# Two matrix-product stages of a two-layer trunk: upper pools on 128-byte multiples, buffers and transposes placed anew

## The chip, the core and the metric

The kernel runs on one core of a Trainium2 chip, in one launch. The metric is the device time of that launch in microseconds (us). The engines are TensorE (PE in the profile; PEld is its loading of stationary operands), VectorE (DVE), ScalarE (ACT), GpSimd (POOL) and SyncE (SP, which issues nearly all DMAs).

## What is computed

One streaming step of a two-layer encoder, for 1024 prompt tokens and 128 sample tokens of width 1024: nine blocks of 128 rows, the ninth being the sample's. Layer 0 (L0) mixes with a gated linear recurrence, layer 1 (L1) with differential attention; each is followed by the same MLP. All is float32.

```python
for l in range(DEPTH):                                    # 2
    a = _rmsnorm(h, norm_g[l, 0])
    m = ...                                               # recurrence or attention, then @ w_o
    h = h + _rmsnorm(m, norm_g[l, 1])
    f = jnp.square(jax.nn.relu(_rmsnorm(h, norm_g[l, 2]) @ w_up[l])) @ w_down[l]   # 1024x4096, 4096x1024
    h = h + _rmsnorm(f, norm_g[l, 3])
```

The attention's own projections read `_rmsnorm(h)` of L0's result; the output of L1 is returned.

## The kernel before

**Products.** Each float32 operand is split in two: a high part in the type fp32r (an ACT cast) and the rest (a DVE subtraction). A product is three matmuls: high by high, high by low, low by high (`mm3`, L228). Wide matmuls have 512 columns, pj and pi 256, pq and pf 384. An operand in the text is named by the tile: h or l at the end is the high or the low part.

**Stages.** On L0: recurrence, `out_proj` (L596), `mlp_up` (L675), `mlp_down` (L851); on L1: attention, `out_proj`, `mlp_up`, `mlp_down`. In the profiled execution they begin at about 0, 630, 760, 1145, 1558, 2140, 2240 and 2622 us.

**Pools.** `Area` (L69) opens one tile pool for each name of a list. Pools without a side are stacked from the low end of the SBUF upwards (lower pools), those with `side="right"` from the high end downwards (upper pools). A pool of a later stage lies over bytes of an earlier one, and a tile's first use waits for the last reader of what it lies over. aTh and aTl (lower, all stages) hold the transposed input of the products, by block; in down they are the places of its operands.

**out_proj** takes the blocks in the order SOON (L0) or LATE (L1): products pm of a block, then its norm (`rstd_of` L184, with rs_v at L193), the residual (hb, loaded and stored by SP), the second norm, transposes of t by PE (`half_T` L225 to L232) whose results ACT and DVE copy out. As soon as blocks j and j+4 are there, `pair_sums` (L660) makes four sums of their halves, on POOL, for the last block on DVE (L667), and transposes one. The last block in both orders is a prompt block (7); the sample (8) stands sixth.

**mlp_up** multiplies by Strassen's scheme with seven products: P1 to P7, 12 matmuls each, over pairs of column tiles, 16 steps i in all. The sums of weights are POOL's (`sums`); `split` makes the stationary operands s0 (raw weights) and s1 (sums), upper, and, from the second step on in turn, s2, lower. Operands A11, A12, A22 and S2 are slices of aTh and aTl, the others (a1, a3, a4) upper tiles that the op `ops` of the first step makes by transposes. `smp` is the sample's product U (24 matmuls of 256 columns). Results (c) go through relu and square to DRAM (u_dr). The order in the first step is written out by hand:

```python
seq = "P1 smp P2 ops P6 P5 P7 P3 P4" if i == 0 else "P1 P6 P2 P5 P7 smp P3 P4"
```

X, Y, Z and U are PSUM tiles in pools of two banks each.

**mlp_down** runs seven passes in the order P1 P2 P5 P3 P6 P7 P4, over 8 chunks c each (4 in P4, whose rest goes block by block). A chunk is 4 blocks x 2 x 3 = 24 matmuls D of 512 columns, in P1, P2, P5 and P3 also 6 matmuls S for the sample. After each chunk the operands of later ones are made: `h_load` (SP, five chunks ahead) and `h_split` (hst to aTh, aTl: ACT L865, DVE L866), `w_load` and `w_split` (wsta, wstb to wh, wl; where the operand is a sum T1 to T4, POOL subtracts first, L934). hst, wh and wl are upper, wsta and aO lower. `evac` (L963) takes the results out of PSUM into aO and aE: ACT in the first four passes, DVE in P6, P7, P4 (L974 to L980), with two sums on POOL in P6.

**finish** (L942) of a block makes norm, residual and store. On L0 it then scales it (ACT, L263) and at once puts 8 transposes S into PE's order, which fill aTh and aTl for the attention. Blocks 0 to 3 are finished at every second chunk of P7, the sample's at the second chunk of P6, blocks 4 to 7 in the second half of P4 right behind their D products. POOL multiplies some of them by the gain gb (L952).

**Attention** begins with the projections pj of the keys, whose weights go through the ring wst, whi, wlo (`load_w` L155, upper; the query weights through the same wst, with a scaling by POOL). PE's order is the order of issue; each engine works its own instructions in order.

Of the kernel before, what the change touches and what calls it, by code (L numbers as in the profile page):

```python
# [19 lines left out]
P = 128  # L20
# [38 lines left out]
LATE = (0, 4, 1, 5, 2, 8, 3, 6, 7)  # L59
SOON = (0, 1, 2, 3, 4, 8, 5, 6, 7)  # L60
# [8 lines left out]
def tile_kernel(ctx, tc, x_prompt, x_sample, cache_k, cache_v, state_hgrn, norm_g, w_hgrn_in,  # L69
# [61 lines left out]
    aTl = glob.tile([P, NB, KT, P], F32R, name="aTl")  # L131
    rings = [ExitStack()]
# [450 lines left out]
    def prepare(ob, b, o_src, osc, gain, pp):  # L583

        nc.sync.dma_start(out=ob, in_=o_src[b * P:(b + 1) * P, :])
        rs = osc(ob, b, pp)
# [9 lines left out]
    def out_proj(w, gains, gain, o_src, osc, g_post, h_old, h_new, g_pre, order, W=None, early={}):  # L596

        keep = ExitStack()
        ts, blk = Area(keep, "ts", "t"), {}
        with ExitStack() as os_:  # L600
# [9 lines left out]
            def prep(b):  # L610
                if b not in early:
                    prepare(block(b), b, o_src, osc, gain, pp)

            order = LATE if early else SOON
# [7 lines left out]
            for b in order:  # L622
# [8 lines left out]
                if early.get(b) is not None:  # L631
                    ss = pp.tile([P, 2], F32, name="ss2")
# [4 lines left out]
                    rs = rstd_of(ss[:, 0:1], 1, 1.0 / D, pp)  # L637
# [4 lines left out]
                else:  # L642
                    rs = rstd_of(sumsq(pm, t, pp), 1, 1.0 / D, pp)
# [5 lines left out]
                pre_norm(hb, g2, t, t, pp, b)  # L649
# [4 lines left out]
                if b < NBP and b ^ NP in done:  # L654
                    pair_sums(blk, b % NP, nc.vector if b == order[-1] else nc.gpsimd)
# [19 lines left out]
    def mlp_up(l, blk, keep):  # L675
        wu = w_up[l].rearrange("(k p) n -> p k n", p=P)
        with ExitStack() as ms, ExitStack() as ls:
            R = Area(ms, "ur", "wst s0h s0l s1h a1h a1l a3h a3l s1l a4h a4l p1 u2 u3 c0 hs", side="right")
            B = Area(ms, "ub", "X Y Z U", space=PSUM)
# [4 lines left out]
            def bank(tag):  # L684
                return B.tile([P, 512], F32, name=tag)
# [80 lines left out]
            tset = split(st, 1, [(r1, ca), (r0, ca)])  # L766
            pend = None
            for i in range(NFP):
                sets = (raw, tset)
                X, Y, Z, U = None, None, None, None  # L770
                nx = None
                C = {}
                seq = "P1 smp P2 ops P6 P5 P7 P3 P4" if i == 0 else "P1 P6 P2 P5 P7 smp P3 P4"
                for op in seq.split():
                    if op == "P1":
# [4 lines left out]
                        nx = load(i + 1) if i + 1 < NFP else None  # L780
                    elif op == "P2":
# [4 lines left out]
                        store(c, "A11", i)  # L786
                    elif op == "ops":
# [62 lines left out]

    def mlp_down(l, g_post, h_old, h_new, last):  # L851
        wd = w_down[l].rearrange("(i s p) n -> s p i n", s=2, p=P)
        NC = NFP // 2
        with ExitStack() as ms:
            L = Area(ms, "dl", "wsta sst ysm aO")
            R = Area(ms, "dr", "aE wstb jk ss rs_v rs_y rs_t hst wh wl gb hb", side="right")
# [3 lines left out]
            ysm = L.tile([P, 2, 512], F32, name="ysm", bufs=1)  # L860
            gp = nc.gpsimd.tensor_tensor
            vt = nc.vector.tensor_tensor

# [10 lines left out]
            def h_load(n):  # L874
# [3 lines left out]
                hraw[n] = st = R.tile([P, 2, HT] if p < 7 else [P, NFP // 2, P], F32, tag="hst", name="hst", bufs=3)  # L878
# [7 lines left out]
            def h_split(n):  # L886
# [8 lines left out]
                if p < 4:  # L895
                    st = L.tile([P, 2, P], F32, name="sst", bufs=2)
# [14 lines left out]
            def w_get(n, c, x):  # L911
                st = (L if x == "a" else R).tile([P, 2, 512], F32, name="wst" + x, bufs=3 if x == "a" else 2)
# [14 lines left out]
            def w_split(m):  # L927
# [12 lines left out]
            gain = []  # L940

            def finish(b, y):  # L942
# [527 lines left out]
```

## Time and profile before

| what | value |
|---|---|
| median of three runs (lowest, highest) | 3015.61 us (3014.43, 3019.21) |
| the profiled execution | 3016.47 us |
| its span | 3014.8 us |
| mean granted clock of PE | 0.978 |
| busy: PE, PEld, DVE, ACT, POOL | 95%, 83%, 62%, 40%, 27% |
| share of PE in the chain that ended last | 85% |

The span is what the profiler saw of the program, from the first instruction to the last; the difference of 1.67 us lies around it. A share is busy time over the span. The granted clock is what the throttle gave of 2.4 GHz: 1 is full speed, and in a stretch a value between 0.5 and 1 is a mix of the two levels 2.4 and 1.2 GHz. The duration printed for a matmul is longer than the distance to the next one's start, since matmuls overlap.

### The profile page before, as it was taken

The numbers are of one execution on the slowest core, as the hardware profiler recorded it, in microseconds if no ns is written. First come the engines' busy times: TensorE is split into PE (matmuls) and PEld (weight loads), VectorE is DVE, ScalarE is ACT, GpSimd is POOL, SyncE is SP. The second block draws the span as 40 slices with busy tenths as digits, with TensorE's granted clock in tenths as the row PEclk, the third lists the DMA queues.
The fourth block names the chain that finished last, engine by engine and source line by source line (L and its number), as shares of the span: only waits on it lengthen the run. The fifth ranks groups of instructions, "written<-read, shape, count | busy, mean of one in ns | idle before, by whom it ended". The sixth has DMA issues, their size and how long they took to land.

```text
span 3014.8 us, 45342 instructions
## 1 busy us (share of the span) xinstructions
PE 2869.3 (95%) x16897; PEld 2500.1 (83%) x16897; DVE 1866.6 (62%) x3440; ACT 1195.5 (40%) x2566; POOL 803.3 (27%) x618
## 2 busy tenths in 40 slices
PE   7999999979899998999779999999989999999997
PEld 7999999968788886888669999998778888788876
DVE  7777777766644445555954665656675444456576
ACT  4232232333433334443444555556533333344432
POOL 1111111101545440114522110111134544302263
PEclk9999999979999999999989999999999999999999
DMA  4111121142243348678732121312323334577866
GB/s 135 53 52 52 52 58 53 56 148 84 76 150 128 125 152 279 193 264 273 259 113 72 53 75 52 91 52 79 125 105 109 134 125 150 192 240 253 266 228 220
DMA packets 337120, 405.27 MB, mean 134 GB/s; under 512 B 21081, under 2 KB 210690, under 8 KB 336898
## 3 DMA queue, kind: packets, MB, share of 16 engines
q1 hardware_dynamic: 336898, 402.37, 40.5%
q8 instruction: 133, 2.18, 0.3%
q14 instruction: 89, 0.73, 0.1%
HBM read 280.12 MB, written 122.16 MB: 133 GB/s over the span
## 4 chain that ended last, share of the span: by engine, by line
PE 85%; DVE 6%; issue 3%; DMA 3%; ACT 2%; POOL 1%; SPq 0%; ACTq 0%; DVEq 0%; POOLq 0%
PE D L228 17%; PE pj L228 10%; PE Y L228 8%; PE Z L228 6%; PE X L228 5%; PE S L228 3%; PE U L228 3%; PE pi L272 2%; PE pi L271 2%; PE pi L273 2%; PE sc L228 2%; PE po L228 2%; PE pm L271 2%; PE pm L273 2%; PE pm L272 2%
## 5 line engine op out<-in xcount | busy, mean ns | idle before, releaser
L228 PE MATMUL D<-wh,aTh 128*128 128x512 f32 x896 | 359.8, 402 | 27.6 <-ACT aTh L865 15.7
L228 PE MATMUL D<-wl,aTh 128*128 128x512 f32 x896 | 358.2, 400 | 6.0 <-DVE rs_v L193 6.0
L228 PE MATMUL D<-wh,aTl 128*128 128x512 f32 x896 | 357.3, 399 | 1.1 <-DVE aTl L866 1.0
L866 DVE TENSOR_TENSOR aTl<-hst,aTh 128x1024 fp32r<-128x1024 f32 x112 | 147.0, 1316 | 213.6 <-ACT aTh L865 209.3
L228 PE MATMUL pj<-whi,aTh 128*128 128x256 f32 x864 | 254.1, 294 | 5.0 <-ACT whi L179 4.7
L228 PE MATMUL pj<-wlo,aTh 128*128 128x256 f32 x864 | 244.1, 283 | 1.3 <-DVE wlo L180 1.3
L228 PE MATMUL pj<-whi,aTl 128*128 128x256 f32 x864 | 243.7, 282 | 0.0
L228 PEld LDWEIGHTS D<-wh,aTh 128*128 128x128 f32 x896 | 170.8, 191 | 71.3 <-ACT aTh L865 16.6
L865 ACT CAST aTh<-hst 128x1024 fp32r<-128x1024 f32 x112 | 117.1, 1046 | 268.0 <-PE D L228 240.1
L228 PEld LDWEIGHTS D<-wl,aTh 128*128 128x128 f32 x896 | 170.9, 191 | 46.9 <-DVE wl L866 6.4
L228 PEld LDWEIGHTS D<-wh,aTl 128*128 128x128 f32 x896 | 170.7, 191 | 44.4 <-DVE aTl L866 2.5
L866 DVE TENSOR_TENSOR wl<-wsta,wh 128x1024 fp32r<-128x1024 f32 x112 | 181.9, 1627 | 30.7 <-ACT wh L865 27.9
L934 POOL TENSOR_TENSOR wsta<-wsta,wstb 128x1024 f32<-128x1024 f32 x48 | 132.6, 2765 | 219.5 <-DMA wsta<-in_w_down_dram 169.8
L228 PEld LDWEIGHTS pj<-whi,aTh 128*128 128x128 f32 x864 | 164.6, 190 | 11.5 <-ACT whi L179 4.9
L271 PE MATMUL pi<-whi,aTh 128*128 128x256 f32 x576 | 166.4, 289 | 0.4 <-ACT sf L413 0.4
L228 PEld LDWEIGHTS pj<-wlo,aTh 128*128 128x128 f32 x864 | 164.4, 190 | 2.6 <-DVE wlo L180 1.9
L272 PE MATMUL pi<-wlo,aTh 128*128 128x256 f32 x576 | 166.1, 288 | 0.0
L273 PE MATMUL pi<-whi,aTl 128*128 128x256 f32 x576 | 165.4, 287 | 0.0
L228 PEld LDWEIGHTS pj<-whi,aTl 128*128 128x128 f32 x864 | 164.0, 190 | 0.0
L743 POOL TENSOR_TENSOR c<-c 128x512 f32<-128x512 f32 x96 | 113.1, 1178 | 169.4 <-ACT c L742 169.1
L742 ACT ACTIVATE c<-c 128x512 f32<-128x512 f32 x96 | 60.7, 633 | 228.9 <-POOL wst L724 113.5
L865 ACT CAST wh<-wsta 128x1024 fp32r<-128x1024 f32 x112 | 116.7, 1046 | 57.3 <-PE D L228 22.0
(469 smaller groups left out, 8002.9 us busy)
## 6 DMA issues: line engine op xcount, KB each, us to landing
u_dr<-c SPq DMA_DIRECT2D x224, 256.0 KB, 4.3
wsta<-in_w_down_dram SPq DMA_DIRECT2D x112, 512.0 KB, 5.1
hst<-u_dr SPq DMA_DIRECT2D x112, 512.0 KB, 4.5
wst<-in_w_up_dram SPq DMA_DIRECT2D x32, 1024.0 KB, 6.3
wstb<-in_w_down_dram SPq DMA_DIRECT2D x32, 512.0 KB, 4.7
t_dr<-wsta SPq DMA_DIRECT2D x32, 512.0 KB, 3.8
wstb<-t_dr SPq DMA_DIRECT2D x32, 512.0 KB, 5.1
h_dr<-hb SPq DMA_DIRECT2D x27, 512.0 KB, 2.6
```

The source lines that it names most:

```text
L228: pin(nc.tensor.matmul(*a, **k))
L271: matmul(out, lh, rh, start=first, stop=False)
L272: matmul(out, lh, rl, start=False, stop=False)
L273: matmul(out, ll, rh, start=False, stop=last)
L742: nc.scalar.activation(c, c, AF.Relu)
L743: nc.gpsimd.tensor_tensor(out=c, in0=c, in1=c, op=ALU.mult)
L865: nc.scalar.copy(h, st)
L866: vt(out=lo, in0=st, in1=h.bitcast(F32), op=ALU.subtract)
L934: gp(out=x, in0=y if n == "T1" else x, in1=x if n == "T1" else y, op=ALU.subtract)
```

## The change

- A tile `edge` of 24 floats (96 bytes) is allocated first among the upper pools, so every later upper pool starts 96 bytes lower.
- `out_proj`: both orders are new and end with the sample (L0: 0 to 8; L1: LATE). The norm's small tiles move from the pools `op` to the pools `ts`, ahead of the tile t; these stay open until the first step of up is over.
- `mlp_up`: the first step's order is `P1 P2 T ops P6 P5 P7 smp P3 P4`; `T` is the split of the sums (before, it stood ahead of the loop) and then the load of the second step's weights. X and U have one bank each, Y and Z three each. The upper pools' list has another order.
- `mlp_down`: hst becomes a lower pool, the first of them; wsta, sst and ysm become upper ones, in another order. The upper pools belong to `rest`, which is closed in the next stage. In passes P7 and P4 (T3, T4) DVE makes the weight subtraction, and in P6 one of the two sums of evac.
- `finish` is called at chunks 1, 4 and 7 of a pass and puts no transposes into PE's order. It scales the block and lists it in `late`; `to_operand` transposes it three chunks later, in the second half of P4 two blocks later. Blocks 6 and 7 aren't scaled there: `left` keeps them, and `next_stage`, called when the attention's pools are opened, scales them into the attention's tile KS1. Their transposes stand in the first head's key projections, one block each.

The diff, cut to its core (left out: the passing of `ts` to the helpers that take the small tiles' pool, the pool lists of the two calls of `out_proj`, and moved names of small tiles):

```diff
@@ -56,8 +56,7 @@
-LATE = (0, 4, 1, 5, 2, 8, 3, 6, 7)
-SOON = (0, 1, 2, 3, 4, 8, 5, 6, 7)
+LATE = (0, 4, 1, 5, 2, 6, 3, 7, 8)
...
@@ -129,6 +128,8 @@
+    edge = ctx.enter_context(tc.tile_pool(name="edge", bufs=1, side="right"))
+    edge.tile([P, 24], F32, name="edge")
...
@@ -596,7 +597,7 @@
-        ts, blk = Area(keep, "ts", "t"), {}
+        ts, blk = Area(keep, "ts", "ss ss8 rs_v rs_y rs_t t"), {}
...
@@ -609,9 +610,9 @@
-            order = LATE if early else SOON
...
+            order = LATE if early else range(NB)
...
@@ -629,30 +630,30 @@
-                    pair_sums(blk, b % NP, nc.vector if b == order[-1] else nc.gpsimd)
+                    pair_sums(blk, b % NP, nc.vector if len(done) == NBP else nc.gpsimd)
...
@@ -675,14 +676,14 @@
-            R = Area(ms, "ur", "wst s0h s0l s1h a1h a1l a3h a3l s1l a4h a4l p1 u2 u3 c0 hs", side="right")
-            B = Area(ms, "ub", "X Y Z U", space=PSUM)
+            R = Area(ms, "ur", "wst s0h s0l s1h s1l a4h a1h a1l a3h a3l a4l p1 u2 u3 c0 hs", side="right")
+            B = Area(ms, "ub", "X U Y Z", space=PSUM)
...
-                return B.tile([P, 512], F32, name=tag)
+                return B.tile([P, 512], F32, name=tag, bufs=1 if tag in "XU" else 3)
...
@@ -763,27 +764,29 @@
-            tset = split(st, 1, [(r1, ca), (r0, ca)])
-            pend = None
+            tset = pend = nx = None
...
-                X, Y, Z, U = None, None, None, None
-                nx = None
...
-                seq = "P1 smp P2 ops P6 P5 P7 P3 P4" if i == 0 else "P1 P6 P2 P5 P7 smp P3 P4"
+                seq = "P1 P2 T ops P6 P5 P7 smp P3 P4" if i == 0 else "P1 P6 P2 P5 P7 smp P3 P4"
...
-                        nx = load(i + 1) if i + 1 < NFP else None
+                        if i > 0:
+                            nx = load(i + 1) if i + 1 < NFP else None
...
+                    elif op == "T":
+                        tset = split(st, 1, [(r1, ca), (r0, ca)])
+                        sets = (raw, tset)
+                        nx = load(1)
...
@@ -848,18 +851,31 @@
+    late, left = [], []
...
+    def to_operand(b, y, bank):
...
+        for c in range(2):
+            half_T(y[:, c] if len(y.shape) > 2 else y[:, c * 512:(c + 1) * 512],
+                   aTh[:, b, 4 * c:4 * c + 4], aTl[:, b, 4 * c:4 * c + 4], transpose, bank)
...
+    rest = ExitStack()
...
-            L = Area(ms, "dl", "wsta sst ysm aO")
-            R = Area(ms, "dr", "aE wstb jk ss rs_v rs_y rs_t hst wh wl gb hb", side="right")
+            L = Area(ms, "dl", "hst aO")
+            R = Area(rest, "dr", "wsta aE gb wstb sst ysm jk wh wl hb ss rs_v rs_y rs_t", side="right")
...
+            def s_bank(name):
+                return B.tile([P, 512], F32, name="S", bufs=2)
...
@@ -875,7 +891,7 @@
-                hraw[n] = st = R.tile([P, 2, HT] if p < 7 else [P, NFP // 2, P], F32, tag="hst", name="hst", bufs=3)
+                hraw[n] = st = L.tile([P, 2, HT] if p < 7 else [P, NFP // 2, P], F32, tag="hst", name="hst", bufs=3)
...
@@ -909,7 +925,7 @@
-                st = (L if x == "a" else R).tile([P, 2, 512], F32, name="wst" + x, bufs=3 if x == "a" else 2)
+                st = R.tile([P, 2, 512], F32, name="wst" + x, bufs=3 if x == "a" else 2)
...
@@ -931,13 +947,13 @@
-                    gp(out=x, in0=y if n == "T1" else x, in1=x if n == "T1" else y, op=ALU.subtract)
+                    (gp if p < 5 else vt)(out=x, in0=y if n == "T1" else x, in1=x if n == "T1" else y, op=ALU.subtract)
...
-            gain = []
+            gain, step = [], [0]
...
@@ -953,12 +969,16 @@
-                if not last:
-                    jk = R.tile([P, 2, 512], BF16, name="jk", bufs=1)
-                    pre_norm(hb, None, jk, y, R, b)
-                    for c in range(2):
-                        half_T(y[:, c], aTh[:, b, 4 * c:4 * c + 4], aTl[:, b, 4 * c:4 * c + 4],
-                               bank=lambda n: B.tile([P, 512], F32, name="S"))
+                if last:
+                    return
+                jk = R.tile([P, 2, 512], BF16, name="jk", bufs=1)
+                ss = sumsq(hb, jk, R)
+                rs = rstd_of(ss, 1, 1.0 / D, R)
+                if b >= NBP - 2 and b < NBP:
+                    left.append((b, hf, rs))
+                    return
+                nc.scalar.activation(y, hb, AF.Copy, scale=rs)
+                late.append((b, y, step[0]))
...
@@ -972,7 +992,7 @@
-                    gp(out=aE[:, 1, j], in0=aE[:, 1, j], in1=aO[:, 0, j], op=ALU.add)
+                    vt(out=aE[:, 1, j], in0=aE[:, 1, j], in1=aO[:, 0, j], op=ALU.add)
...
@@ -993,7 +1013,7 @@
-                    smp = B.tile([P, 512], F32, name="S", bufs=2)
+                    smp = s_bank("S")
...
@@ -1017,7 +1037,10 @@
-                    if todo and c % 2:
+                    step[0] += 1
+                    if late and late[0][2] < step[0] - 2:
+                        to_operand(*late.pop(0)[:2], s_bank)
+                    if todo and c % 3 == 1:
...
@@ -1033,40 +1056,52 @@
+                        while late and late[0][0] < NP + j - 1:
+                            to_operand(*late.pop(0)[:2], s_bank)
...
-        if not last:
-            next_rings()
-            next_banks()
+        if last:
+            rest.close()
...
+    def next_stage(place):
...
+        for i, (b, hf, rs) in enumerate(left):
+            nc.scalar.activation(place[:, i], hf, AF.Copy, scale=rs)
+            late.append((b, place[:, i]))
+        rest.close()
+        next_rings()
+        next_banks()
...
-        ap = Area(as_, "at", "kt q2 k8 KS0 V0 pK KT_s qq pf px ws so Qx KS1 V1")
+        ap = Area(as_, "at", "kt q2 k8 KS0 V0 pK KT_s qq pf px ws so Qx KS1")
+        next_stage(ap.tile([P, 2, D], F32, name="KS1", bufs=1))
+        ap.pool("V1")
...
@@ -1197,6 +1232,8 @@
+                    if h == 0 and late and b > 0:
+                        to_operand(*late.pop(0), ps_aux)
```

## Rows read from the trace of the kernel before

**Rows 1.** Waits of PE over the whole span: total us, times, longest us.

```profile
PE D L228 <- ACT aTh L865: 15.7, 2, 8.8
...
PE S L232 <- ACT aO L263: 12.0, 3, 6.8
PE D L228 <- DVE aO L978: 11.9, 4, 4.7
PE pt L232 <- DVE t L667: 11.5, 2, 5.8
PE S L232 <- ACT aE L263: 9.8, 1, 9.8
...
PE D L228 <- DVE rs_v L193: 6.0, 1, 6.0
```

**Rows 2.** Windows: us, PE PEld DVE ACT POOL busy, granted clock, DMA share, GB/s.

```profile
760.00:800.00 40.00, 29.93 (x155) 24.69 (x153) 31.23 (x43) 17.20 (x30) 19.95 (x14) 0.87 0.14 47
1144.00:1164.00 20.00, 10.19 (x31) 7.28 (x30) 13.37 (x20) 5.77 (x7) 1.69 (x3) 0.66 1.02 376
1444.00:1500.00 56.00, 39.86 (x167) 31.45 (x166) 52.00 (x58) 29.41 (x45) 30.26 (x11) 0.88 0.80 274
1539.00:1575.00 36.00, 17.99 (x96) 15.72 (x95) 19.55 (x36) 15.84 (x29) 7.67 (x4) 0.72 0.42 140
```

**Rows 3.** Timeline of PE in one step of up: start us, us, instruction.

```profile
1049.88 0.39 PE L228 MATMUL Z<-a4h,s1l 128*128 128x512 f32 x1
...
1051.24 0.39 PE L228 MATMUL Z<-a4h,s1l 128*128 128x512 f32 x1
...
1051.93 0.40 PE L228 MATMUL Y<-aTl,s2h 128*128 128x512 f32 x1
...
1054.20 0.40 PE L228 MATMUL Y<-aTh,s2l 128*128 128x512 f32 x1
...
1056.31 0.39 PE L228 MATMUL X<-aTh,s0l 128*128 128x512 f32 x1
```

**Rows 4.** Groups of PE, whole span: count, busy us, mean ns, idle before.

```profile
L228 PE MATMUL D<-wh,aTh 128*128 128x512 f32 x896 | 359.8, 402 | 27.6 <-ACT aTh L865 15.7 <-DVE aO L978 11.9
...
L228 PE MATMUL U<-s2h,aTl 128*128 128x256 f32 x80 | 22.6, 282 | 0.0
L228 PE MATMUL U<-s1h,aTl 128*128 128x256 f32 x80 | 22.4, 280 | 0.0
```

**Rows 5.** Timeline of SP and PE between up and down of L0.

```profile
1147.56 1.58 SPq L883 DMA_DIRECT2D hst<-u_dr  x3
...
1141.04 0.39 PE L228 MATMUL Z<-a4h,s0l 128*128 128x512 f32 x1
```

**Rows 6.** The page: an ACT group, and DMA issues (KB, us to landing).

```profile
L865 ACT CAST wh<-wsta 128x1024 fp32r<-128x1024 f32 x112 | 116.7, 1046 | 57.3 <-PE D L228 22.0
...
wsta<-in_w_down_dram SPq DMA_DIRECT2D x112, 512.0 KB, 5.1
```

**Rows 7.** Groups of DVE from 1424 to 1520 us.

```profile
L866 DVE TENSOR_TENSOR wl<-wsta,wh 128x1024 fp32r<-128x1024 f32 x13 | 28.9, 2224 | 0.0
L866 DVE TENSOR_TENSOR aTl<-hst,aTh 128x1024 fp32r<-128x1024 f32 x14 | 21.3, 1524 | 12.4 <-ACT aTh L865 12.4
...
L978 DVE TENSOR_TENSOR aO<-aO,D 128x512 f32<-128x512 f32 x4 | 2.6, 676 | 0.0
```

**Rows 8.** Timeline of DVE, one such subtraction a little earlier.

```profile
1418.61 1.22 DVE L866 TENSOR_TENSOR wl<-wsta,wh 128x1024 fp32r<-128x1024 f32 x1
```

**Rows 9.** Timeline of PE and POOL between down and attention.

```profile
1541.79 0.39 PE L228 MATMUL D<-wh,aTl 128*128 128x512 f32 x1
...
1547.67 2.34 POOL L952 TENSOR_TENSOR aO<-aO,gb 128x1024 f32<-128x1024 f32 x1 [12.85 <-ACT jk L206]
...
1558.88 0.56 PE L228 MATMUL pj<-whi,aTh 128*128 128x256 f32 x1
...
1567.57 0.58 PE L228 MATMUL pj<-whi,aTh 128*128 128x256 f32 x1 [4.70 <-ACT whi L179]
```

**Rows 10.** Groups of POOL from 1424 to 1520 us.

```profile
L934 POOL TENSOR_TENSOR wsta<-wsta,wstb 128x1024 f32<-128x1024 f32 x13 | 37.9, 2923 | 37.8 <-DMA wsta<-in_w_down_dram 30.0 <-DVE rs_v L193 4.7 <-DMA wstb<-in_w_down_dram 3.1
```

More of the change, by code (lines that the diff above doesn't have):

```diff
@@ L581, in out_weights, with prepare @@
         return W
-    def prepare(ob, b, o_src, osc, gain, pp):
+    def prepare(ob, b, o_src, osc, gain, pp, ts):
         nc.sync.dma_start(out=ob, in_=o_src[b * P:(b + 1) * P, :])
-        rs = osc(ob, b, pp)
+        rs = osc(ob, b, pp, ts)
         ov = ob.rearrange("p (h v) -> p h v", h=8)
@@ L611, in prep @@
                 if b not in early:
-                    prepare(block(b), b, o_src, osc, gain, pp)
-            order = LATE if early else SOON
+                    prepare(block(b), b, o_src, osc, gain, pp, ts)
+            order = LATE if early else range(NB)
             todo = [b for b in order if b not in early]
@@ L631, in out_proj @@
                 if early.get(b) is not None:
-                    ss = pp.tile([P, 2], F32, name="ss2")
+                    ss = ts.tile([P, 2], F32, name="ss", bufs=3)
                     for nh in range(2):
@@ L859, in mlp_down @@
             aE = R.tile([P, 2, NP, 512], F32, name="aE", bufs=1)
-            ysm = L.tile([P, 2, 512], F32, name="ysm", bufs=1)
+            ysm = R.tile([P, 2, 512], F32, name="ysm", bufs=1)
             gp = nc.gpsimd.tensor_tensor
             vt = nc.vector.tensor_tensor
+            def s_bank(name):
+                return B.tile([P, 512], F32, name="S", bufs=2)
             def split(h, lo, st):
@@ L895, in h_split @@
                 if p < 4:
-                    st = L.tile([P, 2, P], F32, name="sst", bufs=2)
+                    st = R.tile([P, 2, P], F32, name="sst", bufs=2)
                     nc.sync.dma_start(out=st, in_=us_dr[l][PASSES[p][3]][2 * c:2 * c + 2].rearrange("q p t -> p q t"))
@@ L1041, in mlp, with scale_heads @@
         mlp_down(l, g_post, h_old, h_new, last)
-        if not last:
-            next_rings()
-            next_banks()
+        if last:
[7 more added lines that the diff above has]
+        next_banks()
     blk, keep = out_proj(w_hgrn_out[0], lambda kr: [gv[:, G_ON + 2 * kr + i:G_ON + 2 * kr + i + 1] for i in range(2)],
-             None, o_dr[0], lambda ob, b, pp: rstd_of(ssh[:, b, :], 8, 1.0 / P, pp), norm_g[0:1, 1], lambda b: rows(xp, xs, b), h_dr[0],
-             norm_g[0:1, 2], "whix5 wlox5 whix6 wlox6 whix7 wlox7 gb hb t8 ss ss8 rs_v rs_y rs_t")
+             None, o_dr[0], lambda ob, b, pp, ts: rstd_of(ssh[:, b, :], 8, 1.0 / P, ts), norm_g[0:1, 1], lambda b: rows(xp, xs, b), h_dr[0],
+             norm_g[0:1, 2], "whix5 wlox5 whix6 wlox6 whix7 wlox7 gb hb t8")
     mlp(0, blk, keep, norm_g[0:1, 3], h_dr[0], h_dr[1], False)
     scaled = set()
-    def scale_heads(ob, b, pp):
+    def scale_heads(ob, b, pp, ts):
         if b < NBP:
@@ L1062, in scale_heads @@
         nc.vector.tensor_tensor(out=jk, in0=ob, in1=ob, op=ALU.mult)
-        ss = pp.tile([P, 8], F32, tag="ss8", name="ss8")
+        ss = ts.tile([P, 8], F32, tag="ss8", name="ss8")
         nc.vector.tensor_reduce(out=ss, in_=jk.rearrange("p (h v) -> p h v", h=8), axis=AX.X, op=ALU.add)
-        return rstd_of(ss, 8, 1.0 / P, pp)
+        return rstd_of(ss, 8, 1.0 / P, ts)
     with ExitStack() as as_:
-        ap = Area(as_, "at", "kt q2 k8 KS0 V0 pK KT_s qq pf px ws so Qx KS1 V1")
+        ap = Area(as_, "at", "kt q2 k8 KS0 V0 pK KT_s qq pf px ws so Qx KS1")
+        next_stage(ap.tile([P, 2, D], F32, name="KS1", bufs=1))
+        ap.pool("V1")
         wk = w_kv.rearrange("(k p) n -> p k n", p=P)
@@ L1440, in tile_kernel @@
              lambda b: h_dr[1][b * P:(b + 1) * P, :], h_dr[2], norm_g[1:2, 2],
-             "whix5 wlox5 whix6 wlox6 whix7 wlox7 gb hb t8 ss ss8 rs_v rs_y rs_t", Wo, early)
+             "whix5 wlox5 whix6 wlox6 whix7 wlox7 gb hb t8", Wo, early)
     mlp(1, blk, keep, norm_g[1:2, 3], h_dr[2], None, True)
```

10 lines of the change are left out of this document (5 added, 5 removed).

## The prediction, made before the changed kernel ran

> **What bounds the kernel now.** The profiled execution took 3016.47 us with a span of 3014.8; its 1.67 us around the span I leave as they are. It stands 0.9 us above the median of the runs, so a sum made against it serves for the median too. PE is busy 95% of the span, so I read first where it waits (PE's own waits) and then the stretches around the long waits with their granted clock. PE's waits show what ends them [rows 1]: the first operands of the down stage, evacuations by DVE, the pair sums of out_proj, and the finished blocks' scaling by ACT. The windows show what they cost [rows 2]: seven joints, each with idle time (length less PE busy) and, behind the idle time, a stretch at 1.2 GHz instead of 2.4. A mean clock of 0.66 over 20 us is 13.6 us at half speed, which costs 6.8 us where PE works. With L0 and L1 for the two layers, idle plus clock: out_proj to up 10.1+5.2 (L0) and 10.0+5.2 (L1); up to down 9.8+6.8 and 7.0+3.4; the passes P7 and P4 of down 16.1+6.7 and 11.5+5.2; down to attention 18.0+10.0. Together 125 us. The rows shown are L0's four stretches; L1's three repeat them.
>
> **Where PE does not wait** it runs one product after another, and there the start-to-start distance counts, not the duration that a row prints. In one stretch of up [rows 3] it is 1.36/6 = 227 ns where both operands come from upper pools (Z<-a4,s1), 2.27/10 = 227 where both come from below (Y<-aTh,s2), and 2.11/9 = 234 where one comes from each side (X<-aTh,s0, from Y's last start on), at the same 512 columns and the same full clock. In the program before, the lower pools lie on multiples of 128 bytes, the upper ones 96 bytes past one. So the pair's relative place within 128 bytes goes with 6 to 7 ns of 234; I take 5.5, since the evicting engines disturb fast pairs as well.
>
> **The change, part by part.**
>
> *The 96-byte tile.* It puts all upper pools on multiples of 128. Each small pool set moved ahead of t adds 384 or 640 bytes, again multiples, so out_proj's lower weights keep theirs. Products of 512 columns with operands from both sides, by the loops: D 3x896 [rows 4], S 384, up 708 a layer = 1416, out_proj with the early halves 540: 5028 x 5.5 ns = 27.7 us. The 1152 products of 384 columns (pq, pf) have no equal pair in the trace: bounds 0 and 1152 x 5.5 = 6.3 us; I take 1.7, since the next narrower form gains nothing. That form, 256 columns (pj, pi; 4320), has one equal pair, U<-s2h at 282 ns beside U<-s1h at 280 [rows 4]: read as steps that is a loss of about 1.2 ns, 5.2 us. The bounds there are +2 ns (8.6 us lost) and -2.8 ns (half of the wide form's gain, 12 us won). Part: 27.7 + 1.7 - 5.2 = **24 us won**, ends 10 and 46. A rule speaks against it: the Trainium skill (SBUF — State Buffer, section on the two separate sides) says that TensorE waits for no one at SBUF, and gives weight loads a read port independent of the moving operand's; by it the part is worth 0. The steps of rows 3 disagree, and it is a rival below.
>
> *Down's first buffers.* hst moves below, over s2h and s2l, which the last up step doesn't read. Before, its three loads were issued at 1147.56 [rows 5], after up's last product, and the first D product waited 8.8 us on their cast. Now they can go about 20 us earlier. But wsta moves up: its first buffer is the lowest of the three and lies over the upper half of s0h, which P3 of the last step reads until 1141.4 [rows 5]. From there: landing 5.1 us and cast 1.05 [rows 6], semaphores 0.2, so 1147.8 against PE free at 1144.9: a wait of 2.9 us stays, and some 2 us of clock. The other bound is 0 (the load comes out of the idle DMA time before). I keep 5 us a layer: 16.6 - 5 + 10.4 - 5 = **17 us won**, ends 8 and 27. Attention's lambda tiles now lie under hb, and run after down instead of in this joint, where DVE spent 3 us on their load: counted in it.
>
> *Sample last, tset later, banks.* The last prompt block's norms, pair sums and transposes get the sample's 48 products (48 x 0.231 = 11.1 us) as cover; the sample's own load, norm and store come last, under P1 and P2 and the S operands, since its up products wait until P7. Moved past them: its h load and store on SP, the two tset casts and subtractions, the 1 MB load of the next weights (needed only five products later, and its one buffer is taken until then). If that cover fails, 10 us a layer stay. But DVE is busy 31.2 of 40 us in this joint [rows 2], and the sample's norm moves into it, so no more than 8.8 can go per layer; I take 7: **14 us won**, ends 4 and 30. X and U have one bank each now; X is written again five products (13 us) after its last reader: nothing.
>
> *Finished blocks.* Before, a block's scaling and transposes stood in PE's order right behind its finish: 9.8 us on ACT aE at 1444 [rows 1, 2]. They now come three chunks later (3 x 24 x 0.231 = 16.6 us), at a finish every third chunk, whose h load and store move with it; T3 and T4 and one add per block leave POOL for DVE. In 1424 to 1520, DVE gains 12 x 1.22 + 4 x 0.68 = 17.4 us. It loses waits: wl took 2224 ns on average there, aTl 1524, against 1.22 us for the same operation beside an idle POOL [rows 7, 8]: 13 x 1.0 + 14 x 0.3 = 17.3 us. DVE therefore stays as full as it was (52 of 56 us), and the wait of P4's first products on DVE aO stays: 6.3 us and its clock, in both layers. L0 wins the 9.8 and most of its clock, 13; L1, without transposes, its 6.0 on DVE less 1, 5: **18 us won**, ends -15 (the subtractions queue behind their loads, in front of the evacuations) and 38.
>
> *Last two blocks in attention.* 16 of the 24 transposes leave the joint, and new weights find their places while down still runs: wst over wsta, free early. But the first whi buffer lies over gb, which block 7's gain product reads. That ended 8 us after the last D product [rows 9] behind ACT's casts of the blocks before; without them I make it 1.0 + 1.3 + 2.4 = 4.8. With cast and subtraction the first pj comes 7.5 us after the last D, not 16.7 [rows 9]. The query weights need that wst buffer again; their first product comes some 7.7 + 4.3 + 2 + 1 = 15 us after the last D (that cast's end, landing, scaling by POOL, cast) instead of 25.4. Won: 10 us of start; the 1.6 us of moved transposes come back later, and the clock still falls once: **10 us won**, ends 0 and 20.
>
> Sum: 24 + 17 + 14 + 18 + 10 = 83; 3016.5 - 83 = **2933**.
>
> **Rivals.** *Joints close altogether*: late loads and transposes find all their cover; 24 + about 92 of the 125: 2900. For it: SP and POOL have room in most joints; against: DVE at 52 of 56. Chance 0.11. *The joints move*: what is freed waits a few us later for DVE, as the P7 row suggests, and of the 59 us a third comes: 3016.5 - 24 - 20 = 2972. Chance 0.17. *Alignment does nothing* (the change doesn't do what its first part is for): the 7 ns come from what else differs between X and Y; 3016.5 - 59 = 2957. Against it: the same split stands with sides exchanged (Z). Chance 0.08; the Trainium skill's rule named above would give this time. *Slower*: T3 and T4 make DVE wait for two loads in its queue, and behind them stand wl, the evacuations and the finishes. POOL waited 33 us for these loads in 1424 to 1520 [rows 10]. If all of that and the added 22 us a layer (16 x 1.22 + 4 x 0.68) land on PE, 2 x 55 = 110 us stand against the other parts' 65: 3062. It decides from 32 us a layer, or 2.7 us per chunk over 12 chunks; four chunks of lookahead speak against it. Chance 0.05.
>
> **Numbers.** The forecast case has 0.59, and reaches by its bounds from 2905 to 2965. With the closed joints, the missing alignment and most of the moved joints, the range 2890 to 2985 leaves 0.2 out. Faster by over 0.2% (6 us, about what a measurement tells from no change) 0.93, within it 0.02, slower 0.05.
>
> **What would show it.** D's and X's steps at 227 to 229 ns, so some 220 D products in 50 us of P1 to P6 and not 216, with pj unchanged within 2 ns; hst issued before 1130 (on before's clock), and D's first wait under 4 us; PE's list without S on ACT aE; P4's wait on DVE aO still there; first pj 7 to 9 us after the last D. Wrong would be: unequal gains between D and up, or new waits of PE on DVE in P7.

## The result and the profile after

The changed kernel takes 2993.2 us (median; 2992.89 to 2994.06), the kernel before 3017.41 in the same comparison: a ratio of 0.9921, 95% interval 0.9904 to 0.9938. It is faster by 24 us; the forecast was 83 us, and its range ended at 2985.

In each trace I take three sums per stretch: the time in which PE has no instruction (idle), half of PE's busy time at 1.2 GHz (what the clock costs), and the rest (work). They are worked out from every PE record and every change of the granted clock; the stretches are bounded by the same products in both traces.

| both layers, us | before: idle + clock | after: idle + clock | won | forecast |
|---|---|---|---|---|
| last pm to the end of up | 22.0 + 6.0 | 21.3 + 9.0 | -2.3 | 14 |
| end of up to the 48th D | 16.8 + 4.8 | 8.5 + 4.8 | 8.3 | 17 |
| P7 and P4 | 27.6 + 7.4 | 14.0 + 4.3 | 16.7 | 18 |
| down to attention (L0) | 18.0 + 5.2 | 15.1 + 4.6 | 3.5 | 10 |
| all other stretches | 61.0 + 11.8 | 61.8 + 12.2 | -1.2 | |
| work, whole program | 2834.1 | 2835.3 | -1.2 | 24 |

The waits of PE in the changed kernel, over the whole span (waited for: total us, times, longest):

```profile
PE pt L233 <- DVE t L266: 10.8, 2, 6.6
PE pj L229 <- ACT whi L180: 9.2, 2, 7.3
...
PE D L229 <- ACT wh L881: 7.3, 2, 4.0
PE D L229 <- DVE aO L998: 6.7, 2, 6.0
PE X L229 <- ACT p L777: 5.9, 2, 5.0
...
PE pj L229 <- DVE wlo L181: 5.5, 2, 2.8
PE D L229 <- DVE aO L994: 3.4, 2, 2.8
```

Against [rows 1], the 9.8 us of S on ACT aE are 1.6 (below the rows shown), those of D on the first operands fell from 15.7 to 7.3, and pair sums are no longer waited for; but the sample's norm (t L266) and the copy of P1's result (p L777) are new, and pj waits longer for its weights (9.2 us for whi, 4.7 before [rows 9]; 5.5 for wlo). The windows that answer to [rows 2] (us, busy time of PE, PEld, DVE, ACT, POOL, granted clock, DMA share, GB/s):

```profile
764.00:802.00 38.00, 28.25 (x139) 23.92 (x138) 30.02 (x42) 16.34 (x29) 11.85 (x9) 0.82 0.15 49
1146.00:1166.00 20.00, 15.54 (x54) 11.76 (x54) 13.88 (x15) 9.84 (x12) 2.29 (x2) 0.83 1.01 367
1424.00:1480.00 56.00, 50.92 (x219) 40.61 (x218) 52.07 (x73) 29.98 (x45) 13.60 (x6) 0.97 0.84 296
1525.00:1561.00 36.00, 20.86 (x129) 19.26 (x127) 21.53 (x44) 18.04 (x30) 11.27 (x14) 0.76 0.44 136
```

The first joint has as little PE as before at a lower clock; the second and third won PE time; DVE is as full in the third as it was (52.07 of 56 us), as forecast.

**The steps.** Two rows of PE's timeline of the changed kernel, first and last of the 12 products X of one P1:

```profile
1034.01 0.40 PE L229 MATMUL X<-aTh,s1h 128*128 128x512 f32 x1
...
1036.58 0.39 PE L229 MATMUL X<-aTh,s1l 128*128 128x512 f32 x1
```

2.57/11 = 234 ns, as before [rows 3], though both operands now lie on multiples of 128 bytes. Over all D at full clock the mean distance from start to start is 232.8 ns after and 233.4 before.

### The profile page after: what moved, and what is told of

It is laid out like the page before. It is cut to its first block, busy times and chain, and to the rows that moved or that the text cites. A ratio compares the mean times of both kernels' runs of the same rounds, so it can differ in the third digit from the quotient of the medians.

```text
span 2990.9 us, 45344 instructions
## 1 busy us (share of the span) xinstructions
PE 2870.2 (96%) x16897; PEld 2508.1 (84%) x16897; DVE 1853.1 (62%) x3480; ACT 1197.8 (40%) x2568; POOL 706.8 (24%) x578
## 4 chain that ended last, share of the span: by engine, by line
PE 38%; DVE 6%; issue 3%; DMA 2%; ACT 2%; POOL 0%; SPq 0%; DVEq 0%; ACTq 0%; POOLq 0%
PE pj L229 10%; PE D L229 8%; PE Y L229 4%; PE Z L229 3%; PE X L229 3%; PE sc L229 2%; PE po L229 2%; PE U L229 2%; PE S L229 1%; DMA wsta<-in_w_down_dram 1%; PE pt L226 1%; DVE wl L882 1%; DVE rs_t L198 1%; DVE hb L970 1%; DVE aTl L882 1%
## 5 line engine op out<-in xcount | busy, mean ns | idle before, releaser
L882 DVE TENSOR_TENSOR wl<-wsta,wh 128x1024 fp32r<-128x1024 f32 x112 | 148.5, 1327 | 30.7 <-ACT wh L881 29.1
L743 ACT ACTIVATE c<-c 128x512 f32<-128x512 f32 x96 | 60.7, 632 | 227.3 <-POOL wst L725 101.0
L1262 POOL COPY qq<-q 128x256 f32<-128x256 f32 x64 | 27.9, 436 | 388.0 <-PE pqT L226 260.7
```

Of the source, the lines that this page charges most:

```text
L743: nc.scalar.activation(c, c, AF.Relu)
L882: vt(out=lo, in0=st, in1=h.bitcast(F32), op=ALU.subtract)
L1262: nc.gpsimd.tensor_copy(qq, view(Qb[h, i][:], (h % 2) * P, [(64, 2), (0, 2), (1, 64)]))
```

## The experiments

The reference for most of them is e1, not the changed kernel. The times of e1, e13 and e14 are medians of four runs, that of e4 of six; every other is one run. Stretches and steps come from one traced execution each.

**Where the operands lie.** e1, e2 and e3 differ from the changed kernel in the edge tile alone.

```diff
-    edge.tile([P, 24], F32, name="edge")
+    edge.tile([P, 56], F32, name="edge")      # e1; [P, 40] in e3, no tile in e2
```

e4 is the kernel before with a tile of 56 floats.

> The changed kernel with the edge tile of 56 floats (224 bytes) in place of 24: upper and lower pools then agree modulo 256 bytes, where the changed kernel has them 128 apart. Theory A (the relative place of the two operands counts modulo 256, not 128): X, Y, Z, D, S and pm of 512 columns step at 227 to 229 ns on average, not 231 to 233, and some 5000 of them win 4 ns each: about 20 us less than the changed kernel, 2973 us; pj and pi of 256 columns may lose about 1 ns, up to 4 us back. Theory B (the place does not matter, the fast pairs of the kernel before were fast for another reason): 2990 to 2996 us, D still at 233 ns on average.

> The changed kernel without the edge tile: upper pools 96 bytes past a multiple of 128, as before. Theory A: no pair of operands from both sides agrees modulo 256 with or without the tile, so nothing is lost: within 4 us of the changed kernel, D at 233 ns on average in both. The prediction's theory (modulo 128 counts): 24 us slower, 3017 us.

> The changed kernel with an edge tile of 40 floats (160 bytes): upper pools a multiple of 64 but not of 128 bytes away from the lower ones. Theory A: again unequal modulo 256, within 4 us of the changed kernel and D at 232 to 234 ns on average. A theory that the size of the tile works through something else than equality (a smooth gain towards 56 floats) expects a D between 229 and 232 ns and 8 to 12 us less.

> The kernel before with nothing but an edge tile of 56 floats ahead of the upper pools. Theory A: the same 20 us as in e1, without any other part of the change: 2995 to 3000 us. Theory B: 3015 us, no change.

Measured: e1 2970.3 us (ratio to before 0.9845, 0.983 to 0.986); e2 2986.95; e3 2971.5; e4 3009.2 (0.9971, 0.9958 to 0.9984). The same P1 rows in e1:

```profile
1034.68 0.39 PE L229 MATMUL X<-aTh,s1h 128*128 128x512 f32 x1
...
1037.17 0.39 PE L229 MATMUL X<-aTh,s1l 128*128 128x512 f32 x1
```

2.49/11 = 226 ns. Sorted by address of the moving operand less that of the next stationary one, modulo 256 (addresses from the built programs, steps from the traces at full clock, single waits left out), the mean steps in ns are:

| difference | 512 columns | 256 columns |
|---|---|---|
| 0 | 227.3 (e1), 228.1 (before) | 119.5 (e1) |
| 64 | 229.4 (e3) | 117.2 (e3) |
| 128 | 232.7 (after) | 118.9 (after) |
| 192 | 233.0 (e3) | |
| 32, 96, 224 | 233.3 to 233.4 (before, e2) | 118.3 (224, before) |

Theory A holds as far as the runs go: places that agree modulo 256 make the fast pair, and the edge tile of the change leaves the operands 128 apart. But every fast pair also agrees modulo 512, since no program here has a difference of 256 modulo 512; whether the period is 256 or 512 is not shown. That the next stationary operand counts, and not the product's own, is seen where products end in the kernel before: 40 steps with an equal own operand and an unequal next one took 235 ns, 40 the other way round 227 to 232. The D step is 226.8 ns in e1. e4 shows the place at work by stage: X falls to 226.8 ns, D stays at 232.7, because the older order of down's upper pools puts wh another 128 bytes off; so e4 won 9 us where 20 were expected. My expectation for e3 was wrong: it was to equal the changed kernel, and took 2971.5. The other theory named there, a smooth gain with the tile's size, has this D step right but not the rest: pairs 192 apart stay at 233.0 in e3, and e4 with e1's tile leaves D at 232.7. A difference of 64 bytes is nearly as good as none for D (229.3 ns), and the best met for the 256 columns of pj and pi; it has a direction (64 and 192 differ). e1's work is 27.3 us below the changed kernel's, its span only 22.2: idle time grew by 5, for instance that of S on aE from 1.6 to 5.4. P7 and P4 alone hold 5.3 us more; that PE only arrives there sooner is my reading, which no run tests apart. e2 ran 6 us below the changed kernel, where Theory A allowed 4, and 3.1 of it are work, all in the recurrence, where 256 and 384 columns step 0.6 and 1.3 ns faster at the old place: the tile of 24 floats lost more in the narrow products than it won in the wide ones.

**The sample's order.** e5 is e1 with the order and the first step of before; e9 also undoes the later split T, e12 also the pair sums' rule. From e12, e15 undoes the banks, e16 the small tiles' place, and e17 both and the order of up's upper pools.

```diff
-LATE = (0, 4, 1, 5, 2, 6, 3, 7, 8)
+LATE = (0, 4, 1, 5, 2, 8, 3, 6, 7)                       # e5; SOON likewise
-                seq = "P1 P2 T ops P6 P5 P7 smp P3 P4" if i == 0 ...
+                seq = "P1 smp P2 T ops P6 P5 P7 P3 P4" if i == 0 ...   # e9, e12: no T, split ahead of the loop
-                    pair_sums(blk, b % NP, nc.vector if len(done) == NBP else nc.gpsimd)
+                    pair_sums(blk, b % NP, nc.vector if b == order[-1] else nc.gpsimd)   # e12
```

> e1 with the orders of before (sample sixth, its products between P1 and P2 of the first step, the split of the sums still behind P2). The prediction's theory (sample last is worth 7 us a layer): the two joints between out_proj and up grow by 14 us in all against e1, 2984 us. Theory C (what is won on the last block's chain is lost on two new waits, of P2 on the copy of P1's result and of the sample's transposes on its norm): within 3 us of e1's 2970; idle time of the L0 joint 9 to 11 us in both.

> e5, and the split of the sums ahead of the loop again with the next weights' load behind P1, so that the whole part on the sample is undone but for the small tiles' place and the banks. If the part as a whole is worth the 14 us of the prediction: 2984 us as e5. Theory D (the later split T costs what the order wins, since DVE then has s1l to make in the middle of the joint): 2972 to 2977 us, and the two joints' idle and clock like those of before.

> e9 with the sums of the last pair on DVE again (e5 and e9 had kept the changed kernel's rule, by which the reordered last pair went to POOL: PE waits 4.1 us for it in each layer there). If order, split and load are worth nothing together: 2968 to 2973 us, like e1's 2970. If they are worth the 9 us between e9 and e1 after all: 2977 to 2981 us.

> e12 with two banks each for X, Y, Z and U as before. e12's two joints still stand 7 us above those of before in idle time and clock. If the banks (X and U one each) cost that, this kernel is some 6 us below e12: 2970 us. If it is the small tiles or the upper pools' order: within 2 us of e12.

> e12 with the norm's small tiles back in out_proj's own pools. If the small tiles' place (ahead of t, kept into up) costs the 7 us: 2970 us. If it is worth something, as it was put there: above 2978 us.

> e12 with banks, small tiles and the order of up's upper pools as before, so that out_proj and up are those of the kernel before but for the 256-byte place. The joints then have the idle time and clock of before: 2968 to 2971 us, and the whole part is worth -2 to 2 us against e1. If it stays at 2976, what is lost in the joints comes from the place of the pools and not from this part.

Whole times: e5 2983.89, e9 2979.42, e12 2976.56, e15 2976.98, e16 2972.78, e17 2975.61. Since other stretches move by some us as well, I compare the length of out_proj, joint and up of both layers together: before 985.6, after 986.9, e1 975.3, e5 984.8, e9 984.4, e12 982.5, e15 982.8, e16 977.1, e17 976.9. So the whole part is worth 1.6 us (e17 against e1) and not 14; e1 and e8, which are the same program (below), differ by 1.4 us here, so even the 1.6 is not clear of nothing. The expectations for e5 and e9 missed it, because both kept a rule that sends the reordered last pair to POOL; e15 shows nothing for the banks; with the old order the small tiles' new place costs 5.4 us (e16 against e12, one execution each), which may be why e12 looked like a gain of the order. e17's total stands 5.3 us over e1's, 3.7 of it outside these stretches; I leave it open.

Where the cover went is seen in the changed kernel. Timeline rows of ACT and PE in the L0 joint:

```profile
770.86 1.04 ACT L708 CAST s1h<-wst 128x1024 fp32r<-128x1024 f32 x1 [2.54 <-POOL wst L726]
771.81 0.58 ACT L777 COPY p<-X 128x512 f32<-128x512 f32 x1
```

```profile
772.44 0.79 PE L229 MATMUL X<-aTh,s0h 128*128 128x512 f32 x1 [5.00 <-ACT p L777]
...
782.88 1.94 PE L233 MATMUL pt<-ident,t 128*128 128x128 f32 x8 [4.20 <-DVE t L266]
```

P2 adds to the bank that P1's result is copied from. Without the sample's products between them, PE waits for the copy, which stands in ACT's order behind a cast of the weight sums, and that one waits for POOL. Then the sample's transposes stand in PE's order in front of the operands that were ready. e6 puts the casts behind the copy; e7 also puts the transposes behind the operands:

```diff
+                    tc.add_manual_dep(cast.ins, p1c.ins.name, ...)     # e6, casts of T only
...
                         s_ops("S4", lambda j: blk[j][:, 512:D])
+                        for c in range(2):                              # e7
+                            half_T(blk[NBP][:, c * 512:(c + 1) * 512], aTh[:, NBP, 4 * c:4 * c + 4],
+                                   aTl[:, NBP, 4 * c:4 * c + 4], transpose, lambda n: bank("YZ"[c]))
```

> e1 with the casts of the sums (s1h) bound to come behind the copy of P1's result on ACT, in the first step only. Theory C: the 5.1 us wait of X on ACT in L0 falls to under 1 us; but PE then meets the wait on the sample's norm earlier, so 0 to 4 us are won in all, 2967 to 2970 us. A theory that the copy is late for its own sake (PE's products end late) keeps the wait.

> e6, and the sample's transposes put behind the operands S1, S3 and S4 in PE's order (the sample's block kept until then, hs made lower to find room). Theory C: the waits of pt on t (4.2 us in L0, 6.3 us in L1 in e1) go with it, since 8 us of transposes now stand in front: 4 to 8 us less than e1 in both joints together, 2962 to 2966 us. If DVE's load alone sets the joints (31 of 40 us busy before), the wait turns up at the operands instead, and under 2 us are won.

e6 2967.12, e7 2957.38. The wait on the copy in L0 is 1.2 us in e6, and the transposes of the last pair are waited for next, so out_proj, joint and up together shrink by only 0.5 us; in e7 they take 966.8, 8.5 less than in e1 and 10.1 less than in e17. The waits of PE that e7 keeps in its L0 joint:

```profile
762.41 0.50 PE L229 MATMUL X<-aTh,s0h 128*128 128x512 f32 x1 [1.19 <-ACT p L782]
...
771.81 1.09 PE L233 MATMUL pt<-ident,t 128*128 128x128 f32 x4 [6.39 <-DVE rs_v L194]
```

In the kernel before it waits there twice as well, with the sample's product U on t and then with the last pair's transposes:

```profile
767.27 0.36 PE L228 MATMUL U<-s0h,aTh 128*128 128x256 f32 x1 [3.00 <-DVE t L644]
...
781.62 1.09 PE L232 MATMUL pt<-ident,t 128*128 128x128 f32 x4 [5.79 <-DVE t L667]
```

Another 5.5 us of e7's gain are idle time at the start of the first out_proj, where the wait on the first block's load fell from 13.1 to 6.3 us: in SP's order the loads now stand elsewhere. I had not meant that.

**The start of down.** e8 takes one unused tile, which was to keep the first wsta from lying over s0h.

```diff
+            R.tile([P, 2, 512], F32, name="wsta", bufs=3)
             for n in range(5):
                 h_load(n)
```

> e1 with one unused wsta tile taken at the start of down, so that the first real one lies over the weights' staging tile, free early, and not over s0. The prediction's theory (the first D waits because the first wsta lies over what P3 reads): the first load is issued some 10 us earlier, the waits of D on wh (5.2 us in L0, 3.6 us in L1 in e1) go to under 1 us, and with their clock 8 to 11 us are won: 2960 us. If the loads would not come sooner anyway: no change.

The edit does nothing: an unused tile takes no buffer, and the built program of e8 is that of e1, instruction for instruction and address for address, with the first wsta over s0h as before. So its 2974.12 us are a fifth run of e1 (the others: 2969.90 to 2974.85), and its waits of D, 4.6 us in L0 and 4.9 in L1 against e1's 5.2 and 3.6, show how far two executions of one program differ. In the changed kernel the load starts when P3 has ended, as forecast (rows of SP, PE and ACT):

```profile
1143.46 0.99 SPq L929 DMA_DIRECT2D wsta<-in_w_down_dram  x2
```

```profile
1143.27 0.40 PE L229 MATMUL Z<-a4h,s0l 128*128 128x512 f32 x1
```

```profile
1149.58 1.04 ACT L881 CAST wh<-wsta 128x1024 fp32r<-128x1024 f32 x1 [4.52 <-DMA wsta<-in_w_down_dram]
```

In e8, being e1, it does the same, behind a store of the last step in SP's order:

```profile
1136.82 0.33 SPq L747 DMA_DIRECT2D u_dr<-c  x1
1137.68 0.99 SPq L929 DMA_DIRECT2D wsta<-in_w_down_dram  x2
```

The forecast's reason, the overlap with s0h, fits these rows; no run takes it away, so it is not shown against the rival, SP's order. The next experiment speaks to that one.

**Three joints at once.** e10 is e7 with three edits: gb moved, T3 and T4 on POOL again, the first two wsta loads issued by ACT (with e8's tile).

```diff
-            R = Area(rest, "dr", "wsta aE gb wstb sst ...
+            R = Area(rest, "dr", "wsta aE wstb gb sst ...
-                    (gp if p < 5 else vt)(out=x, ...
+                    gp(out=x, ...
-                nc.sync.dma_start(out=st, in_=w_src(n, c))
+                (nc.scalar if n == "B11" and c < 2 and not Wop else nc.sync).dma_start(out=st, in_=w_src(n, c))
```

> e7 with three edits, each in a joint of its own. (1) The gain tile gb placed so that the first whi of the attention lies over a wstb buffer: if the wait for gb's last product holds the first pj, it comes 3 us after the last D instead of 7, and the later waits on wlo shrink too: 4 us won between down and attention; if ACT's order (norms of blocks 6 and 7 ahead of the cast) holds it, 1 us. (2) T3 and T4 subtracted by POOL again: if the waiting subtraction in front of P6's and P7's evacuations makes the waits of D on aO (3.3 us in L0, 7.0 us in L1), these go to under 2 us and 6 us are won in P7 and P4; if POOL's slowing of DVE weighs more, 5 us are lost. (3) The first two wsta loads issued by ACT, over the weights' staging tile: if SP's order (the loads behind stores that wait for the last step's results) made e8's wait, D's first waits (4.6 and 4.3 us) fall to under 1 us and with the clock 8 us are won.

2970.26 us, 13 more than e7. The unused tile takes no buffer here either, so the first wsta lies over s0h as before. Its waits of PE:

```profile
PE D L229 <- DVE aO L1006: 16.3, 2, 8.4
PE D L229 <- ACT wh L889: 12.3, 2, 6.7
PE pj L229 <- DVE wlo L181: 11.3, 2, 8.7
```

(1) Between down and attention the first pj came without a wait and the next waited 8.7 us for wlo; the stretch won 2.0 us. (2) P7 and P4 together took 6.1 us longer in L0 and 2.6 in L1. That isn't POOL's subtraction alone: e14 below, which moves gb too but lets DVE subtract, lost 6.8 and 1.9 us there against e13. With POOL stands the wait of P4's first products on aO in L0 (8.4 us; 1.0 in e7, 1.8 in e14), against a P7 that was 3.7 us shorter than e7's. Whether DVE's subtraction is a gain as a whole isn't shown. (3) ACT issued the first load 3.1 us ahead of the end of up's products, right behind the last product of P3 and no sooner than SP in e1 (3.2 us); that stretch lost 2.9 us, little more than the 1.9 by which e1 and e8 differ. So SP's order isn't what holds the load until P3's end, and the overlap with s0h, which stands in all these programs, remains as its reason.

**Pools 64 bytes off where products are narrow.** e11 and e13 move up's and down's pools by 16 floats more than the others, e14 adds e10's gb and POOL's subtraction for the first head's key weights.

```diff
-    edge.tile([P, 56], F32, name="edge")
+    edge.tile([P, 40], F32, name="edge")
-            R = Area(ms, "ur", "wst s0h ...
+            R = Area(ms, "ur", "wst pad s0h ...          # e13, e14; "pad wst s0h" in e11 (on e10)
-                                     4, 2 * P, gains=gs))
+                                     4, 2 * P, gains=gs, eng=nc.gpsimd if h == 0 else None))   # e14
```

> e10 with upper pools 64 bytes past a multiple of 256 in the recurrence, the attention and out_proj, and on multiples of 256 in up and down only (an edge tile of 40 floats and a tile of 16 floats ahead of up's and down's upper pools). Theory A with e3's steps (256 columns: 117.2 ns at 64 bytes, 119.4 ns at equality): pi and pj lose 2.2 ns each, 4320 x 2.2 = 9.5 us less than e10, with D, X and Y still at 227 ns. If the wide products of out_proj and attention lose as much: no difference.

> e7 with upper pools 64 bytes past a multiple of 256 outside up and down, as in e11, but with the 16 floats behind wst and wsta, so that these lie exactly over the staging buffers that are free early. Theory E (e11 lost 13 us at the joints out_proj to up because the shifted staging tile reached into weights that out_proj reads to its end): the joints are back at e7's, the 256-column steps at 117 ns stay, and 7 us are won: 2950 us. If the shift itself costs the joints: 2960 us or more.

> e13 with gb moved as in e10 and the low parts of the first head's key weights made by POOL. In e10 the first pj came with the end of down and the second waited 8.7 us for wlo, which DVE made behind the norms of blocks 6 and 7. If that order on DVE is the wait: with POOL the wlo wait falls to under 4 us, and 5 to 7 us are won between down and attention: 2944 us. If POOL's subtractions come as late: within 2 us of e13.

e11 2976.0: pi and pj step at 117 ns and work fell by 8.3 us, but out_proj, joint and up lost 12.2 us against e10's. e13, where the pad stands behind the staging tile, so that this lies over the earlier staging buffers alone, builds on e7 and took **2949.59 us** (ratio to before 0.9771, 0.9755 to 0.9786), with those joints as in e7: 44 us less than the changed kernel, the fastest of all. e14 took 2958.73 (its traced execution 2963.14): pj waits for the same weights on POOL, and the query weights come after them.

```profile
PE pj L229 <- ACT whi L180: 9.0, 1, 9.0
...
PE pj L229 <- POOL wlo L181: 6.4, 1, 6.4
```

But that stretch is only about 2 of the 13.3 us by which e14's traced execution is longer than e13's; 8.7 stand in P7 and P4. With gb moved, the place of the first key weights is free early, and in L0 ACT casts them in P4, ahead of a block's sum of squares; the transposes S of a block then wait 4.3 us for its scaling, as in e10, where it is 1.9 in e7 and e13 (rows of ACT and of PE in e14):

```profile
1494.39 2.01 ACT L180 CAST whi<-wst 128x1024 fp32r<-128x1024 f32 x2
1496.29 1.06 ACT L207 ACTIVATE jk<-aO 128x1024 bf16<-128x1024 f32 x1
```

```profile
1501.84 1.97 PE L226 MATMUL S<-ident,aO 128*128 128x128 f32 x8 [4.26 <-ACT aO L990]
```

## Why the prediction was wrong

The measured 2993.2 us are near what two of the rivals give together, which the prediction priced only apart: nothing from the tile, and a third of the joints' 59 us (3016.5 - 20 = 2996.5).

**The 96-byte tile (24 us, got none).** The step that failed is "the pair's relative place within 128 bytes goes with 6 to 7 ns of 234". The fast pairs of [rows 3] agree modulo 512, and so modulo 256 and 128 as well; the trace of before has no pair 128 apart and could not tell these, and I took the smallest. The mechanism and its size were right (e1: 27 us of work), for another tile; the reason given for 5.5 ns in place of 6 to 7, that evicting engines disturb fast pairs, no run tests (over the whole trace of before the two kinds of pairs differ by 5.3). The same step has "384 or 640 bytes, again multiples" wrong: they are 128 off modulo 256, and some 300 products pm step at 232.7 ns even in e1. The part's low end of 10 us was not what its bounds give either (27.7 + 0 - 8.6 = 19). Its rival "alignment does nothing" described this part's outcome for the wrong reason, and the Trainium skill's rule that I set against it (SBUF — State Buffer, the section on the two separate sides), which I read as saying that the place doesn't matter, doesn't agree with e1 in that reading: 226 ns against 234 for the same product. The expected loss at 256 columns was there: 0.4 to 0.6 ns per product after, 1.1 to 1.2 in e1.

**The clock in all joints.** "Idle plus clock" came to 125 us, with 42.5 for the clock. I had taken the whole stretch at 1.2 GHz as lost; but in the window of 1144 to 1164 [rows 2] PE works for only 10.2 of 20 us, and a wait costs the same at either clock. Counted over busy time, the clock cost 23.4 us in those joints. And it hardly fell: 35.2 us in the whole program before, 34.9 after. A shorter wait was still followed by a stretch at 1.2 GHz.

**Down's first buffers (17, got 8.3).** The step "2.9 us stays" was close: 4.0 and 3.3 us, the load landing after 6.1 us instead of 5.1. hst goes early as forecast (1124.25). What was mis-sized is the clock: 4.8 us of cost before and after, where I had 10 and let 6 of them vanish.

**Sample last (14, lost 2.3).** "The last prompt block's norms, pair sums and transposes get the sample's 48 products" as cover left out two things: the sample's 24 products U, moved behind P7, had been the cover of P1's copy, and the transposes of a late sample stand ahead of PE's next work. e7, which repairs both, wins 10.1 us against e17, not the whole 14. DVE's load, which I named as the limit, is 30.0 of 38 us after, as before.

**Finished blocks (18, got 16.7).** Right in size, and by most of its steps: S on aE 1.6 us instead of 9.8; DVE as full as before; P4's wait on aO still 6.0 us in L1. That the sum is so close is partly luck: in L0 the wait that was to stay fell from 6.3 us to 0.7, and new waits, on an evacuation (2.8 us) and on ACT aO (1.6), took some of that back. The subtractions are faster, where [rows 7] had 1524 and 2224 ns (groups of DVE from 1424 to 1520):

```profile
L882 DVE TENSOR_TENSOR aTl<-hst,aTh 128x1024 fp32r<-128x1024 f32 x14 | 19.5, 1394 | 0.4 <-ACT aTh L881 0.4
L882 DVE TENSOR_TENSOR wl<-wsta,wh 128x1024 fp32r<-128x1024 f32 x14 | 18.7, 1338 | 0.0
```

The rival's mechanism may be there in small: an evacuation stands in DVE's order behind a subtraction that starts late, though the profile names no load that it waited for (rows of DVE at the end of P6; PE's wait of 2.8 us is on this evacuation).

```profile
1428.06 1.23 DVE L950 TENSOR_TENSOR wsta<-wsta,wstb 128x1024 f32<-128x1024 f32 x1 [1.89 <-issue]
1429.20 0.68 DVE L994 TENSOR_TENSOR aO<-aO,D 128x512 f32<-128x512 f32 x1
```

**Last two blocks (10, got 3.5).** The first pj came 8.9 us after the last D's end, where it was 16.7 before [rows 9] and 7.5 in the forecast (timeline of PE):

```profile
1526.35 0.40 PE L229 MATMUL D<-wh,aTl 128*128 128x512 f32 x1
...
1535.62 0.58 PE L229 MATMUL pj<-whi,aTh 128*128 128x256 f32 x1 [7.33 <-ACT whi L180]
...
1538.93 0.58 PE L229 MATMUL pj<-wlo,aTh 128*128 128x256 f32 x1 [2.73 <-DVE wlo L181]
...
1545.59 0.39 PE L229 MATMUL pj<-whi,aTh 128*128 128x256 f32 x1 [1.86 <-ACT whi L180]
```

That start was within the forecast's 7 to 9. What failed is the step "15 us after the last D" for the query weights (18.8 us, the last row), and a wait in between that I had left out, on the low part of the first weights: DVE makes it behind the norm of block 7, whose sum of squares ACT works behind two casts (rows of ACT and of DVE).

```profile
1536.41 1.05 ACT L207 ACTIVATE jk<-hb 128x1024 bf16<-128x1024 f32 x1
```

```profile
1537.59 0.15 DVE L194 TENSOR_SCALAR rs_v<-ss 128x1 f32<-128x1 f32 x1 [2.44 <-ACT jk L207]
1537.66 2.35 DVE L181 TENSOR_TENSOR wlo<-wst,whi 128x1024 fp32r<-128x1024 f32 x2
```

e10 shows that gb's product isn't all that sets the joint: there the first pj had no wait, and the second 8.7 us. DVE's order isn't all either: e14 took the low parts off DVE, and its joint was about 2 us longer than e13's.

## What to carry to other kernels

Before two operands are moved to agree at some power of two, find pairs in the trace that agree at that one and not at the next; if there are none, the step is worth a one-line run and not a forecast. When an edit is meant to move a tile, read its address in the built program before the time: e8's tile moved nothing. When work is moved because it covers a wait, list first what it covers at its old place, and what stands behind it in its engine's order at the new one. Half clock costs only where the engine works, and a shorter wait may leave it as it was.

## What was not expected of the hardware

The step of a 512-column fp32r matmul goes with the difference between its moving operand's SBUF address and that of the next stationary operand: 227 ns where they agree modulo 512, 229 at 64 modulo 256, 233 at 128, 192 and at places that are no multiple of 64; a difference of 256 was not run. With 256 columns 64 bytes is the best met (117.2 ns) and equality the worst (119.5). In e13, where most stages have their better place, this is worth 33.3 us of work against the kernel before (2834.1 to 2800.8).
